# Merge steps dealt at 1.1 a product instead of 2.5, and their dependent transfers moved from the sync queue to GpSimd's queue

## The chip, the cores and the metric

The kernel runs on one core of a Trainium2 chip. The core has five engines that run their own instruction streams in order and meet through semaphores: TensorE (PE in the profile: matmuls; PEld: its weight loads), VectorE (DVE), ScalarE (ACT), GpSimd (POOL) and SyncE (SP, which here only issues transfers). Transfers are issued from an engine's queue (SP's, ACT's or GpSimd's) and carried by 16 DMA engines. The metric is the device time of one execution in microseconds, the median of several runs.

## The reference, cut to what matters

One layer of a decoder step over 1024 prompt tokens and 8 x 4 sample tokens, width 1024, all in float32: an RMS norm, one wide input projection, a gated convolution branch (A), a gated delta-rule branch (B) with 8 heads, two output projections, sigmoid gates, a last projection and a norm. The part that the change touches is in branch B. For each head the tokens are cut in chunks, and each chunk needs the inverse of a unit lower triangular matrix before the chunk-by-chunk scan can start:

```python
M = jnp.where(strict, jnp.einsum('bhnik,bhnjk->bhnij', kb, k) * L, 0.0)
eye = jnp.broadcast_to(jnp.eye(C, dtype=M.dtype), M.shape)
Tm = lax.linalg.triangular_solve(eye + M, eye, left_side=True, lower=True)
u_pre = jnp.einsum('bhnij,bhnjv->bhniv', Tm, vb)
w_dec = jnp.einsum('bhnij,bhnjk->bhnik', Tm, kb * jnp.exp(gc)[..., None])
...
def step(S, inp):
    qd, aqk, kd, up, wd, dl = inp
    u = up - jnp.einsum('bhck,bhkv->bhcv', wd, S)
    o = jnp.einsum('bhck,bhkv->bhcv', qd, S) + jnp.einsum('bhij,bhjv->bhiv', aqk, u)
    S = S * dl[..., None, None] + jnp.einsum('bhck,bhcv->bhkv', kd, u)
    return S, o
```

## The kernel before, in words

The kernel uses chunks of 128 tokens (8 of them) and handles the heads in two groups of 4. First come the norm and the projections of q, k, v and part of the output gate (L287, plain products in three float32r passes). Then the other projections run in pairs of column blocks: `project_pair` computes two blocks in seven smaller products instead of eight. Such a *product* is 24 matmuls of 264 columns (L325). There are 25 pairs, so 175 products: one pair of output gates, four of `C_GB`, sixteen of branch A (`branch_a`), four of `C_GA`. Each product needs a split weight tile `w2`, made by ScalarE (L208) and VectorE (L209) from `wr`, a 512 KB weight tile that SP's queue loads (L174, two per pair, three buffers). `take` prepares the tiles of the next two products ahead. At the end come the two output projections (L287 again) and the last projection with the final norm (L1318).

Beside the products runs the chain of branch B, written as Python generators. `pump`, called after every product, adds `rate[0]` to a credit and takes one generator step per whole credit. `chain` runs four stages one after the other:

- `invert` (two generators, one per head group): inverts the 32 x 32 diagonal blocks on VectorE (L619, L620), then stores them in DRAM (L627, L628, L634, SP's queue).
- `merge` (again one per group): puts the 32-blocks together to 64-blocks and these to 128-blocks, per group in 8 + 8 rounds of two steps. In the first half a round loads `lm`, `lh`, `ll` (L645 to L647), does a small matmul (L671), negates it (L673), a second one (L677), copies it to `xx` (L679) and stores it in the DRAM tensor `tscr` (L682, two transfers). In the second half a round loads `m64` (L652), `rh` and the block-diagonal tile `bd` from `tscr` (L656, L657, two transfers each: these depend on what L627 and L682 stored), does a matmul and two transposes (L693, L695), evacuates them (L697, L699), a second matmul (L703), a copy to `x12` (L705) and a store to `tscr` (L707, two transfers). Loads run one round ahead, through two buffers.
- `scan`: the 8 chunks in order, per group; loads `kt`, `qd`, `av`, `tt`, `kd`, `aqk`, `sz` and stores the output, all on GpSimd's queue (L1107, L1172; `aux` is that queue).
- `sample`: the sample tokens, with `state_in` loads (L965), small matmuls (L1021), state updates (L1091, L1096) and stores (L1098), also on GpSimd's queue.

`rate[0]` is 2.5 from the first product on (L1211) and 1.25 from the scan on (L1204). What is left of the chain is run dry before the last pair (L1221).

The order that is written by these calls isn't the last one: a scheduler that works on estimated times reorders each engine's instructions where dependences allow it. So the program's order on an engine is read from the built program, below.

GpSimd also does one multiplication of branch A (L937, L941) between ScalarE's silu (L954) and VectorE's product with it (L947, L952), and clears and copies the rim of the convolution tile (L907, L909, L926, L927).

Of the kernel before, what the change touches and what calls it, by code (L numbers as in the profile page):

```python
# [31 lines left out]
Q4 = 32  # L32
# [19 lines left out]
def hybrid_step(ctx, tc, x_prompt, x_sample, state_conv_a, state_conv_qkv, state_delta, w_in, conv_a_w,  # L52
                conv_b_w, a_log, dt_bias, onorm_w, w_out_a, w_out_b, w_o, norm_w, final_norm_w,
                y_prompt, y_sample, nca_p, ncq_p, nd_p, nca_s, ncq_s, nd_s):
    nc = tc.nc
    pe, act, dve, pool = nc.tensor, nc.scalar, nc.vector, nc.gpsimd
    aux = nc.gpsimd
# [3 lines left out]
    def opened(**kw):  # L61
        st = ExitStack()
        return st, st.enter_context(tc.tile_pool(reuse_waits="tile", **kw))
# [31 lines left out]
    tscr = dram.tile([2, P, NCH, GH, P], F32, name="tscr")  # L95
# [158 lines left out]
    rate, credit = [1.0], [0.0]  # L254
# [382 lines left out]
    def merge(g, pl):  # L637

        ps_ = potile if g else dtile
        bv = bscr[g].rearrange("(b x c h) a j -> x c (h a) b j", b=2, x=2, c=NCH)  # L640

        def load32(c):
            lm, ll = (pl.tile([P, 2, P], F32, tag=f"{nm}{g}", name=nm, bufs=2) for nm in ("lm", "ll"))
            lh = pl.tile([P, 2, Q4], F32, tag=f"lh{g}", name="lh", bufs=2)
            nc.sync.dma_start(lm, lmscr[g, c])  # L645
            nc.sync.dma_start(lh, bv[1, c])
            nc.sync.dma_start(ll, llscr[g, c])  # L647
            return lm, ll, lh

        def load64(c):  # L650
            m64 = pl.tile([P, 2, P], F32, tag=f"m64{g}", name="m64", bufs=2)
            nc.sync.dma_start(m64, m64scr[g, c])  # L652
            rh = pl.tile([P, 2, 64], F32, tag=f"rh{g}", name="rh", bufs=2)
            for i in range(2):
                half_ = slice(i * 64, (i + 1) * 64)
                nc.sync.dma_start(rh[half_], tscr[g, 64:128, c, i::2, 64:128])  # L656
                nc.sync.dma_start(t1[c % 2][half_, :, half_], tscr[g, 0:64, c, i::2, 0:64])  # L657
            return m64, rh, t1[c % 2]

        nxt = load32(0)  # L660
        t1 = [pl.tile([P, 2, P], F32, name=f"bd{g}{i}") for i in range(2)]
        for t in t1:
            pool.memset(t, 0.0)
        yield
        for c in range(NCH):
            lm, ll, lh = nxt
            if c + 1 < NCH:
                nxt = load32(c + 1)
            pw = ps_()
            for b in range(2):  # L670
                pe.matmul(pw[:, b * Q4:(b + 1) * Q4], lhsT=lm[:, b, :], rhs=lh[:, b, :], start=True, stop=True)  # L671
            ww = pl.tile([P, 2, Q4], F32, tag=f"ww{g}", name="ww")
            dve.tensor_scalar(ww, pw[:, 0:64].rearrange("p (b j) -> p b j", b=2), -1.0, None, op0=ALU.mult)  # L673
            yield
            px = ps_()
            for b in range(2):
                pe.matmul(px[:, b * Q4:(b + 1) * Q4], lhsT=ll[:, b, :], rhs=ww[:, b, :], start=True, stop=True)  # L677
            xx = pl.tile([P, 2, Q4], F32, tag=f"xx{g}", name="xx", bufs=2)
            dve.tensor_copy(xx, px[:, 0:64].rearrange("p (b j) -> p b j", b=2))  # L679
            for b in range(2):  # L680
                o = b * 64
                nc.sync.dma_start(tscr[g, o:o + Q4, c, :, o + Q4:o + 64].rearrange("a h j -> h a j"),  # L682
                              xx[:, b, :])
            yield
        nxt = load64(0)
        yield
        for c in range(NCH):
            m64, rh, tb = nxt
            if c + 1 < NCH:
                nxt = load64(c + 1)  # L690
            pw = ps_()
            for i in range(2):
                pe.matmul(pw[:, i * 64:(i + 1) * 64], lhsT=m64[:, i, :], rhs=rh[:, i, :], start=True, stop=True)  # L693
            for i in range(2):
                pe.transpose(pw[:, P + i * P:2 * P + i * P], tb[:, i, :], ident)  # L695
            w64 = pl.tile([P, 2, 64], F32, tag=f"w64{g}", name="w64")
            dve.tensor_scalar(w64, pw[:, 0:P].rearrange("p (i j) -> p i j", i=2), -1.0, None, op0=ALU.mult)  # L697
            t11 = pl.tile([P, 2, P], F32, tag=f"t11{g}", name="t11")
            act.copy(t11, pw[:, P:3 * P].rearrange("p (i j) -> p i j", i=2))  # L699
            yield  # L700
            px = ps_()
            for i in range(2):
                pe.matmul(px[:, i * 64:(i + 1) * 64], lhsT=t11[:, i, :], rhs=w64[:, i, :], start=True, stop=True)  # L703
            x12 = pl.tile([P, 2, 64], F32, tag=f"x12{g}", name="x12")
            dve.tensor_copy(x12, px[:, 0:P].rearrange("p (i j) -> p i j", i=2))  # L705
            for i in range(2):
                nc.sync.dma_start(tscr[g, 0:64, c, i::2, 64:128], x12[i * 64:(i + 1) * 64])  # L707
            yield

    def potile():  # L710
# [481 lines left out]
    def chain():  # L1192
        for nm, fn in (("iv", invert), ("mg", merge)):
            held, pl = opened(name=nm, bufs=1, side="right")
            live = [fn(g, pl) for g in range(2)]
            while live:
                for one in list(live):
                    try:
                        next(one)
                        yield  # L1200
                    except StopIteration:
                        live.remove(one)
            held.close()
        rate[0] = 1.25  # L1204
        for nm, fn in (("cp", scan), ("sp", sample)):
            held, pl = opened(name=nm, bufs=1, side="right")
            yield from fn(pl)
            held.close()

    background.append(chain())  # L1210
    rate[0] = 2.5  # L1211
    by_pair(C_BZ, 6, AF.Silu, put_z)
# [18 lines left out]
    def htile(pl, nm, n=TT):  # L1231
        return pl.tile([P, n], F32R, tag="h", name=nm)
# [46 lines left out]
    for e in range(KC):  # L1279
        sg = gate_in(gbscr, e)  # L1280
        m = ma[e]
        a, b_ = htile(ha, "mh"), htile(ha, "ml")
# [16 lines left out]
    for k in range(KC):  # L1299
        a, b_ = htile(hb, "woh", D), htile(hb, "wol", D)  # L1300
# [61 lines left out]
```

## Time and profile before

| | us |
|---|---|
| median of 3 runs | 1531.49 (1530.23 to 1535.01) |
| profiled execution | 1535.13 |
| span of its instructions | 1533.4 |
| TensorE busy (matmul) | 1428.1 (93%) |
| VectorE / ScalarE / GpSimd busy | 801.1 / 551.6 / 329.9 |
| mean granted TensorE clock | 0.949 of 2.4 GHz |

The profile is one execution. A view by stretches gives for each engine how long it was busy and, in brackets, how many instructions it began there; PEclk is the clock granted to TensorE as a share of 2.4 GHz. In the timeline an instruction's row ends, where the engine was idle before it, with that idle time and what ended it. "SPq" rows are the issue of transfers on SP's queue; their duration is the time that the issue took, not that of the transfer.

### The profile page before, as it was taken

Reading aid. Unit: us, or ns where it says so; the run is one execution under the profiler, and the core shown is the slowest. Engines: PE = TensorE matmul, PEld = TensorE weight load, DVE = VectorE, ACT = ScalarE, POOL = GpSimd, SP = SyncE. Lnnn points to the kernel's source line nnn. Section 1 sums busy time; section 2 is a strip of 40 time slices with the busy share of each in tenths; the row PEclk is TensorE's granted clock in tenths of the full one; section 3 lists DMA queues with packets and bytes.
Section 4 is the critical chain, followed back from the end, with each engine's and each line's share of the span. In section 5 each row is a group of like instructions: output and inputs, shape, how many; then the busy total and the mean of one; then the engine's idle time right before and its main releaser. Section 6 shows DMA issues by size and latency. Waiting matters only on the chain. (4 is left out here: it accounts for less than half of the span.)

```text
span 1533.4 us, 24570 instructions
## 1 busy us (share of the span) xinstructions
PE 1428.1 (93%) x9673; PEld 1366.6 (89%) x9673; DVE 801.1 (52%) x1456; ACT 551.6 (36%) x1184; POOL 329.9 (22%) x485
## 2 busy tenths in 40 slices
PE   5999898999999998656999999998799999999998
PEld 3899898999999998546999999997799999999885
DVE  6255554435469993213565566467655463255422
ACT  5265564546534431002444444122234460122211
POOL 2032332223211000002565543216200000000200
PEclk9999999999999999557999999799999999999999
DMA  6177656555572345335676564424622283232511
GB/s 192 33 164 209 194 154 191 147 130 145 150 178 85 92 121 144 91 96 157 187 200 200 177 196 137 125 75 143 202 71 86 99 295 112 84 125 86 180 41 45
DMA packets 243077, 212.29 MB, mean 138 GB/s; under 512 B 61417, under 2 KB 215930, under 8 KB 242962
## 3 DMA queue, kind: packets, MB, share of 16 engines
q1 hardware_dynamic: 222272, 143.59, 33.4%
q0 software_dynamic: 17616, 60.37, 13.0%
q10 hardware_dynamic: 3074, 6.77, 1.3%
q8 instruction: 76, 1.25, 0.3%
q14 instruction: 39, 0.32, 0.1%
HBM read 138.12 MB, written 72.56 MB: 137 GB/s over the span
## 5 line engine op out<-in xcount | busy, mean ns | idle before, releaser
L325 PE MATMUL pb<-uh,w 128*128 128x264 f32 x1600 | 315.0, 294 | 17.1 <-ACT w L208 13.7
L325 PEld LDWEIGHTS pb<-uh,w 128*128 128x128 f32 x1600 | 257.6, 194 | 22.7 <-ACT w L208 14.5
L287 PE MATMUL pp<-uh,wl 128*128 128x352 f32 (+1 forms) x744 | 242.9, 326 | 13.5 <-DVE wl L190 13.5
L287 PE MATMUL pp<-uh,wh 128*128 128x352 f32 (+1 forms) x744 | 249.8, 336 | 0.2 <-ACT ext L406 0.2
L287 PE MATMUL pp<-ul,wh 128*128 128x352 f32 (+1 forms) x744 | 242.6, 326 | 0.0
L325 PE MATMUL pb<-ul,w 128*128 128x264 f32 x800 | 233.8, 292 | 0.0
L325 PEld LDWEIGHTS pb<-ul,w 128*128 128x128 f32 x800 | 155.3, 194 | 1.8 <-issue 1.8
L287 PEld LDWEIGHTS pp<-uh,wl 128*128 128x128 f32 (+1 forms) x744 | 140.0, 188 | 17.6 <-DVE wl L190 15.2
L287 PEld LDWEIGHTS pp<-uh,wh 128*128 128x128 f32 (+1 forms) x744 | 139.6, 188 | 4.0 <-issue 0.8
L287 PEld LDWEIGHTS pp<-ul,wh 128*128 128x128 f32 (+1 forms) x744 | 139.9, 188 | 2.0 <-issue 0.5
L208 ACT CAST w<-s 128x512 fp32r<-128x512 f32 x100 | 61.4, 620 | 149.3 <-PE pb L325 65.9
L418 DVE SCALAR_TENSOR_TENSOR cv<-ext,vecT,cv 128x1080 f32<-128x1080 f32 x72 | 99.5, 1386 | 10.1 <-ACT cv L416 8.7
L209 DVE TENSOR_TENSOR w<-s,w 128x512 fp32r<-128x512 f32 x100 | 75.0, 752 | 40.5 <-ACT w L208 39.1
L188 ACT CAST wh<-wr 128x1024 fp32r<-128x1024 f32 (+1 forms) x47 | 48.7, 1036 | 106.8 <-PE pp L287 104.5
L325 PE MATMUL pb<-t4h,w 128*128 128x264 f32 x400 | 81.0, 300 | 6.5 <-DVE p L949 6.5
L209 DVE TENSOR_TENSOR w<-wr,w 128x512 fp32r<-128x512 f32 x75 | 53.0, 709 | 50.9 <-ACT w L208 50.8
L190 DVE TENSOR_TENSOR wl<-wr,wh 128x1024 fp32r<-128x1024 f32 (+1 forms) x47 | 59.8, 1273 | 37.0 <-ACT wh L188 35.5
L325 PE MATMUL pb<-t7h,w 128*128 128x264 f32 x400 | 76.7, 289 | 0.0
L325 PE MATMUL pb<-t6h,w 128*128 128x264 f32 x400 | 76.4, 287 | 0.0
L325 PEld LDWEIGHTS pb<-t4h,w 128*128 128x128 f32 x400 | 65.9, 199 | 7.4 <-issue 7.4
L208 ACT CAST w<-wr 128x512 fp32r<-128x512 f32 x75 | 46.7, 623 | 49.0 <-PE pb L325 44.2
L325 PEld LDWEIGHTS pb<-t7h,w 128*128 128x128 f32 x400 | 63.2, 191 | 0.0
(362 smaller groups left out, 3082.0 us busy)
## 6 DMA issues: line engine op xcount, KB each, us to landing
wr<-in_w_in_dram SPq DMA_DIRECT2D x80, 512.0 KB
scr<-pk SPq DMA_DIRECT2D x16, 768.0 KB
sb<-in_state_delta_dram POOLq DMA_DIRECT2D x16, 512.0 KB, 4.4
zscr<-zt SPq DMA_DIRECT2D x8, 528.0 KB
gbscr<-zt SPq DMA_DIRECT2D x8, 528.0 KB
yscr<-za SPq DMA_DIRECT2D x8, 528.0 KB
gascr<-zt SPq DMA_DIRECT2D x8, 528.0 KB
sg<-gascr POOLq DMA_DIRECT2D x8, 528.0 KB, 4.0
```

What stands on the lines that cost most here:

```text
L188: act.copy(wh, wr)
L190: dve.tensor_tensor(wl, wr, wh.bitcast(F32), op=ALU.subtract)
L208: act.copy(w2[:, 0], src)
L209: dve.tensor_tensor(w2[:, 1], src, w2[:, 0].bitcast(F32), op=ALU.subtract)
L287: pe.matmul(ps[:a.shape[2], :BLK], lhsT=a[:, k, :], rhs=m[k][:, sl], start=(k == 0 and i == 0), stop=(k == KC - 1 and i == 2))
L325: pe.matmul(ps[:, g, :QT], lhsT=a[:, k, :], rhs=m[:, k, sl], start=start and k == 0 and i == 0, stop=(k == 3 and i == 2), skip_group_check ...
L418: dve.scalar_tensor_tensor(cv, ext[:, j:j + LB], vecT[:, j * 24 + ci:j * 24 + ci + 1], cv, op0=ALU.mult, op1=ALU.add)
```

## The change

The rate is set where a stage of the chain begins: 2.5 for `invert`, 1.1 for `merge` (1.25 for the scan and the sample tokens, as before). In `merge` the transfers that store to `tscr` (L682, L707) and the loads that read what such a store wrote (L656, L657) go to GpSimd's queue; `lm`, `lh`, `ll` and `m64` stay on SP's. From L1195 on lines have one number more than before.

```diff
             rh = pl.tile([P, 2, 64], F32, tag=f"rh{g}", name="rh", bufs=2)
             for i in range(2):
                 half_ = slice(i * 64, (i + 1) * 64)
-                nc.sync.dma_start(rh[half_], tscr[g, 64:128, c, i::2, 64:128])
-                nc.sync.dma_start(t1[c % 2][half_, :, half_], tscr[g, 0:64, c, i::2, 0:64])
+                aux.dma_start(rh[half_], tscr[g, 64:128, c, i::2, 64:128])
+                aux.dma_start(t1[c % 2][half_, :, half_], tscr[g, 0:64, c, i::2, 0:64])
...
-                nc.sync.dma_start(tscr[g, o:o + Q4, c, :, o + Q4:o + 64].rearrange("a h j -> h a j"),
+                aux.dma_start(tscr[g, o:o + Q4, c, :, o + Q4:o + 64].rearrange("a h j -> h a j"),
                               xx[:, b, :])
...
-                nc.sync.dma_start(tscr[g, 0:64, c, i::2, 64:128], x12[i * 64:(i + 1) * 64])
+                aux.dma_start(tscr[g, 0:64, c, i::2, 64:128], x12[i * 64:(i + 1) * 64])
...
             held, pl = opened(name=nm, bufs=1, side="right")
+            rate[0] = 2.5 if fn is invert else 1.1
             live = [fn(g, pl) for g in range(2)]
```

**SP's queue, after the stores of `invert`.** Before: the weight tile `wr` for the next pair, then a store of a projection, then the loads of the merges begin.

```order
L634 DMA llscr<-xt 8x32x32 x8
L174 DMA wr<-in_w_in_dram 128x8x128
L1214 DMA gbscr<-zt 128x1056
L645 DMA lm<-lmscr 128x256
L646 DMA lh<-bscr 128x2x32
L647 DMA ll<-llscr 128x256
```

The next weight tile of before stands in the second half of the merges:

```order
L657 DMA bd_5230<-tscr 64x2x64
L656 DMA rh<-tscr 64x2x64
L657 DMA bd_5230<-tscr 64x2x64
L1214 DMA gbscr<-zt 128x1056
L174 DMA wr<-in_w_in_dram 128x8x128
L652 DMA m_6427<-m64scr 128x256
L656 DMA rh<-tscr 64x2x64
```

With the change the same queue has the next weight tile after the first five rounds' loads:

```order
L645 DMA lm<-lmscr 128x256
L646 DMA lh<-bscr 128x2x32
L1215 DMA gbscr<-zt 128x1056
L174 DMA wr<-in_w_in_dram 128x8x128
L645 DMA lm<-lmscr 128x256
L647 DMA ll<-llscr 128x256
```

Between the first of these weight loads and the next, 153 transfers are issued before, and 16 with the change; from there to the end of the merges there are never more than 20 between two.

**TensorE, second half of the merges.** Before, the last first-half rounds and most second-half rounds follow one another with no product between (`pd` and `po` are PSUM tiles of group 0 and group 1, `w64` and `t11` the evacuated results):

```order
L677 MATMUL pd_5911<-ww_5875,ll_5806 128x32 x2
L671 MATMUL po_5906<-lh_5818,lm_5816 128x32 x2
L677 MATMUL po_5948<-ww_5909,ll_5817 128x32 x2
L693 MATMUL pd_6014<-rh_5957,m64_5955 128x64 x2
L695 MATMUL pd_6014<-ident_79,bd00_5229 128x128 x2
L703 MATMUL pd_6069<-w64_6019,t11_6021 128x64 x2
L693 MATMUL po_6030<-rh_5964,m64_5962 128x64 x2
L695 MATMUL po_6030<-ident_79,bd10_5277 128x128 x2
```

With the change the second-half rounds stand between products (L325):

```order
L325 MATMUL pb1_6674<-ul0_121,w2_6586 128x264
L703 MATMUL po_6708<-w64_6628,t11_6630 128x64 x2
L693 MATMUL pd_6752<-rh_6572,m64_6570 128x64 x2
L695 MATMUL pd_6752<-ident_79,bd01_5230 128x128 x2
L693 MATMUL po_6799<-rh_6618,m64_6616 128x64 x2
L695 MATMUL po_6799<-ident_79,bd11_5278 128x128 x2
L325 MATMUL pb1_6674<-t6h_4099,w2_6677 128x264 x2
```

The merges begin at the 37th product in both. They end at the 43rd product before and at the 76th with the change; the scan's first matmul stands in the 46th and in the 82nd, and the last state update of `sample` in the 126th and in the 161st of the 175.

**GpSimd's queue, start of the merges.** Before, nothing of the merges is there:

```order
L663 MEMSET bd_5278 128x256
L907 MEMSET exta 128x2
L909 COPY exta<-pasta 128x8x2
L926 COPY newa<-exta 128x2
L927 COPY newa<-exta 128x16
L907 MEMSET exta 128x2
L909 COPY exta<-pasta 128x8x2
L1107 DMA kt<-scr 128x4x128
```

With the change:

```order
L663 MEMSET bd_5278 128x256
L907 MEMSET exta 128x2
L909 COPY exta<-pasta 128x8x2
L682 DMA tscr<-xx 4x32x32 x4
L657 DMA bd_5229<-tscr 64x2x64 x2
L682 DMA tscr<-xx 4x32x32 x2
L656 DMA rh<-tscr 64x2x64 x2
L657 DMA bd_5277<-tscr 64x2x64
L682 DMA tscr<-xx 4x32x32 x2
L657 DMA bd_5277<-tscr 64x2x64
L656 DMA rh<-tscr 64x2x64 x2
L682 DMA tscr<-xx 4x32x32 x4
```

The stretch of the merges on this queue holds 128 of their transfers and, between them, 21 instructions of branch A.

## Rows read from the trace of the kernel before

**Rows 1.** The page: busy tenths of TensorE, granted clock, in 40 slices.
```profile
PE   5999898999999998656999999998799999999998
PEclk9999999999999999557999999799999999999999
```

**Rows 2.** By stretches: us, busy us (instructions) of each engine, clock, DMA share, GB/s.
```profile
587.80:617.90 30.10, 30.10 (x233) 29.82 (x233) 13.08 (x35) 4.69 (x9) 1.01 (x4) 0.91 0.49 126
632.00:685.00 53.00, 27.57 (x110) 22.36 (x110) 5.74 (x21) 4.71 (x12) 0.00 (x0) 0.50 0.34 87
730.00:940.00 210.00, 208.78 (x1768) 208.34 (x1767) 122.08 (x260) 93.39 (x278) 116.20 (x155) 1.00 0.64 189
940.00:1100.00 160.00, 154.35 (x1072) 143.55 (x1072) 107.83 (x247) 37.62 (x61) 51.86 (x55) 0.91 0.42 124
1100.00:1120.00 20.00, 13.51 (x92) 13.32 (x91) 8.71 (x12) 3.54 (x6) 2.26 (x3) 0.83 0.57 198
```

**Rows 3.** Timeline of SP's queue around the merges: start, duration, instruction.
```profile
581.68 0.41 SPq L174 DMA_DIRECT2D wr<-in_w_in_dram  x1
...
663.57 2.56 SPq L707 DMA_DIRECT2D tscr<-x  x4
...
672.72 2.56 SPq L707 DMA_DIRECT2D tscr<-x  x4
...
679.22 0.43 SPq L174 DMA_DIRECT2D wr<-in_w_in_dram  x1
```

**Rows 4.** Timeline of TensorE around the merges.
```profile
587.74 0.59 PE L325 MATMUL pb<-uh,w 128*128 128x264 f32 x1 [6.18 <-ACT w L208]
...
670.52 1.09 PE L693 MATMUL pd<-rh,m 128*128 128x64 f32 x4 [2.53 <-DMA rh<-tscr]
...
690.74 0.55 PE L703 MATMUL po<-w,t 128*128 128x64 f32 x4
691.29 0.63 PE L693 MATMUL pd<-rh,m 128*128 128x64 f32 x4
691.93 0.41 PE L695 MATMUL pd<-ident,bd 128*128 128x128 f32 x2
...
712.86 0.59 PE L325 MATMUL pb<-uh,w 128*128 128x264 f32 x1 [5.30 <-ACT w L208]
```

**Rows 5.** Stretches, instructions of L325 alone: us, PE busy (count), PEld, clock, DMA.
```profile
594.00:616.00 22.00, 17.17 (x117) 14.96 (x117) 1.00 0.41 99
1160.00:1220.00 60.00, 60.00 (x496) 60.00 (x495) 1.00 0.32 102
581.50:712.80 131.30, 27.91 (x169) 24.53 (x168) 0.65 0.45 116
```

**Rows 6.** The same of 594 to 616, L671 alone, then L677 alone.
```profile
594.00:616.00 22.00, 4.90 (x36) 4.49 (x35) 1.00 0.41 99
594.00:616.00 22.00, 4.82 (x36) 4.80 (x36) 1.00 0.41 99
```

**Rows 7.** GpSimd's transfers: issue in ns (min/median/max); last row, landing of L1172's.
```profile
L1107 POOL DMA_DIRECT2D kt<-scr x16: 747/750/854, 629.4 to 906.3; - x16
L1107 POOL DMA_DIRECT2D tt<-tscr x16: 549/578/627, 704.2 to 912.8; - x16
L1063 POOL DMA_DIRECT2D oscr<-osm x1: 952/952/952, 1040.3 to 1040.3; - x1
DMA to landing us min/median/max: 2.8/3.8/5.8
```

**Rows 8.** Who waited for whom on GpSimd, whole span.
```profile
POOL qd L1107 <- DMA rh<-tscr: 72.4, 1, 72.4
...
POOL sz L1107 <- DMA oscr<-sz: 12.4, 9, 2.5
```

**Rows 9.** Timeline of GpSimd: the multiplication of branch A.
```profile
733.70 1.78 POOL L937 TENSOR_TENSOR za<-za,cv 128x528 f32<-128x528 f32 x1 [0.77 <-ACT za L954]
```

## The prediction

> **What bounds the kernel now.** I read the slices of the page first: TensorE is busy for nine tenths or more nearly everywhere, with one long hole from about 610 to 730 us, and in the same slices the granted clock is halved [rows 1]. So TensorE bounds the kernel, and the question is what the hole holds. The view by stretches cuts it: from 632 to 685 us TensorE is busy 27.6 of 53.0 us at a clock of 0.50, so at 1.2 instead of 2.4 GHz, while the DMA engines are busy only a third of the time [rows 2]. SP's timeline names the holder. A weight tile is issued at 581.68 and the next one at 679.22, 97.5 us later [rows 3]; the order has 153 transfers between them, 0.64 us each, so the queue is full all that time. In the second half of the merges one round of both groups (two `m64`, eight loads, four stores) takes 672.72 - 663.57 = 9.15 us of issue [rows 3]. TensorE, in order, meets a round's matmul and waits for its `rh` (2.53 us in the row shown). Its timeline also shows the ends of the stretch: products wait for their weights until 587.74, after 6.18 us, and again until 712.86, after 5.30 us [rows 4]. Between these lie 131.3 us that hold 169 matmuls of products, seven products and one matmul [rows 5]. After it, from 730 to 940 us, TensorE does products and scan steps at full clock and is busy 208.8 of 210 us [rows 2]: a chain dealt beside products can run without a gap.
>
> **What the change takes away.** The work of the 131.3 us stays; I price it at full clock.
>
> - Products: 60.0 us hold 496 matmuls of L325 where nothing else runs, 0.121 us each [rows 5]. 169 x 0.121 = 20.4 us.
> - First-half matmuls: 594 to 616 us ran at full clock with 117 matmuls of L325, 14.2 us; the other 7.8 us carried 36 + 36 rows of L671 and L677, 18 steps of four rows [rows 5, 6]. 0.435 us a step, 32 steps: 13.9 us.
> - Second-half matmuls: at full clock L703 took 690.74 to 691.29, 0.55 us, and L693 with L695 until 692.34, 1.05 us [rows 4]. Sixteen times 1.60: 25.6 us.
> - The wait of 6.2 us before 587.74 stays: the weight tile that ends it stands behind the same stores of `invert` in both programs.
> - The half clock just after that wait stays: from 587.8 to 617.9 us the granted clock was 0.91 [rows 2], which takes 0.09 x 30.1 = 2.7 us.
>
> Sum: 68.8 us. What goes is 131.3 - 68.8 = 62.5 us. It needs both parts. The rate spreads the merges from the 37th to the 76th product, and the queue's part gives SP back to the weights: no more than 20 transfers, some 13 us at 0.64, between two weight loads.
>
> A rule of the Trainium skill speaks against the second part: "DMA: Bandwidth & Descriptors", section "Issuing engines are not separate DMA queues", says that all queues feed the same 16 DMA engines, so that a second issuing engine only saves issue time, usually a small thing. By that rule alone the queue's part would bring next to nothing. Here the trace differs: issue filled SP's queue for 97.5 us [rows 3] with the DMA engines a third busy [rows 2], so issue time is what is saved.
>
> **What it adds.** 128 transfers on GpSimd's queue. Its trace shows none of this shape; a transfer with 128 rows (`tt`) took 0.58 us to issue, one with 512 rows 0.75, the dearest shown 0.95 [rows 7]. These have 128 rows each, so I take 0.58: 74 us in all, with 0 and 0.95 as ends (122 us). TensorE's own work from the 37th to the 76th product is 40 x 2.91 (24 x 0.121) + 13.9 + 25.6 = 156 us, so the queue is half full. It also carries branch A's multiplications there, six at up to 1.8 us [rows 9]. Stretch 730 to 940 is the nearest row for such a mixture: GpSimd 116 of 210 us busy, TensorE without a gap [rows 2].
>
> The queue works in order, and a load that depends on a store waits on it until the store has landed, 3.8 us after issue [rows 7]. Behind the waiting load stand the next stores, and behind those VectorE's copies to `xx`, which has two buffers a group; behind these PSUM tiles and TensorE. The order exposes one full landing wait, at the first `bd` load; from then on five to nine transfers (3 to 5 us) lie between a store and its load. So one wait is certain, and its delay can reach the first rounds, which TensorE still takes close together. Low end 0, as from 730 to 940; high end one landing for each of six reused buffers, 23 us. I take 5: one landing and a little. In the second half `rh` is loaded six to ten products (17 to 29 us) ahead, no wait.
>
> The scan and the sample tokens move 35 products later, unchanged among themselves. `sample` cost TensorE 5.7 us of idle from 940 to 1100 and 6.5 just after [rows 2]; it now ends beside the `C_GA` pairs, where VectorE has less to do. It may save these 12 us or, with other stores on SP's queue, cost as much again; I take 0. The chain still ends at the 161st product, seven ahead of where it would be run dry.
>
> **Sum.** 1535.1 (the profiled execution, 1.7 us outside the span) - 62.5 + 5 = 1477.6. The profiled execution is 3.6 us above the median of the runs, so 1474.0 on their scale. The forecast's own range: 1535.1 - 62.5 - 12 - 3.6 = 1457 to 1535.1 - 62.5 + 23 + 12 - 3.6 = 1504.
>
> **Rivals.** *GpSimd's queue becomes the chain, and it ends slower.* Place: the first half of the merges. If each of the 16 stores of a round must land before the queue goes on, that is 16 x 3.8 = 61 us, plus the 44 issues that stand there at 0.58, 26: 87 us against TensorE's 12 x 2.91 + 13.9 = 49. TensorE waits 38 us, drops to half clock as it did from 632 to 685, and its 49 us take 98: 1474 - 5 + 38 + 49 = 1556. It decides if most landings are waited for in full. For it: GpSimd has waited on landings, 12.4 us in nine waits in the scan [rows 8]; the 72.4 us there were SP's [rows 8]. Against: the distances in the order.
>
> *VectorE slows GpSimd's issue.* If GpSimd could issue only while VectorE is idle (58% busy from 730 to 940 [rows 2]), 0.58 becomes 1.38 us, 128 of them 177 and branch A's 10: 187 against 156, so 31 us of waits, 1500. Against: `kt` took 747 to 854 ns in just that stretch, hardly any spread [rows 7]. The Trainium skill, "SBUF — State Buffer", section "Who interferes with whom", says that VectorE's copies in two-port modes lock GpSimd out while it writes descriptors; the trace shows at most 0.1 us of that.
>
> *Weights stay late.* SP still has 64 loads of the merges, which wait for buffers in order. If every pair from the 43rd product to the 84th loses what the wait of 5.3 us and its half clock (2.7) cost: 6 x 8 = 48 us, 1522. Both loads of each pair: 1570. Against: no load in front of a weight tile waits for a matmul later than the weight's own place.
>
> *The steps only move.* If the chain can't finish in time, `sample`'s state updates run without products. Before they stand beside the 118th to the 126th product, 8 x 2.91 = 23 us that would be uncovered: 1497. The order, with the last of them at the 161st product, speaks against it.
>
> **Chances.** Forecast 0.78; GpSimd's chain 0.05; VectorE's lock 0.05; late weights 0.08 (a quarter of it with both loads, slower, and a quarter between, no change); moved only 0.04. A measurement can tell 0.3%, 4.6 us. Faster: 0.78 + 0.05 + 0.04 + 0.04 = 0.91, less 0.01 for ends of these beyond; no change 0.03; slower 0.07. The range 1457 to 1504 holds the forecast and two rivals, over 8 in 10.
>
> **What would show it.** Right: no gap of more than 35 us between weight loads on SP's queue; TensorE's clock at 1.0 from 600 us on until the sample stage; no waits of L693 on `rh` and of L703 on its evacuation; L1107's first scan rows near 790 us; GpSimd's issues of L656, L657, L682 and L707 at about 0.58 us. Wrong: waits of L671 or L677 on VectorE's L679, and these on landings; GpSimd rows above 1.2 us; L208 waiting for weights at every pair; VectorE's L947 or L952 waiting for L937.

## The result, and the profile after

The changed kernel took 1458.91 us (median of 3 runs, 1457.01 to 1459.33) against 1531.49: a ratio of 0.9518, 95% interval 0.9490 to 0.9546. It lies inside the range given, near its lower end, 15 us below the forecast. In the profiled executions the span fell from 1533.4 to 1457.2 us, 76.2 us where the sum had 57.5.

The slices of the changed kernel, in which nothing is left of the hole and of the halved clock beside it [rows 1]:

```profile
PE   4999898998999999899999999999999899999998
PEclk8999999999999999999999999999999999999999
```

The view by stretches of the changed kernel, for the stretches of [rows 2]. The columns are the length, the busy time of PE, PEld, DVE, ACT and POOL with the instructions begun, the granted clock, the DMA engines' share and GB/s:

```profile
587.80:617.90 30.10, 25.60 (x192) 24.64 (x193) 15.35 (x38) 6.36 (x11) 16.20 (x26) 0.89 1.00 254
632.00:685.00 53.00, 52.31 (x438) 51.96 (x438) 29.12 (x55) 17.82 (x32) 31.90 (x54) 1.00 0.39 94
730.00:940.00 210.00, 206.35 (x1734) 206.16 (x1733) 119.54 (x247) 87.99 (x250) 116.51 (x161) 0.99 0.63 180
940.00:1100.00 160.00, 159.44 (x1218) 151.91 (x1217) 102.75 (x242) 50.44 (x106) 57.71 (x62) 0.97 0.48 142
1100.00:1120.00 20.00, 19.61 (x139) 17.13 (x138) 11.85 (x28) 6.37 (x11) 7.33 (x7) 1.00 0.74 240
```

In the stretch from 632 to 685 us TensorE was busy 27.6 of 53.0 us at a clock of 0.50; it is now busy 52.3 at 1.00, and begins 438 matmuls there.

SP's timeline of the changed kernel, weight tiles alone, where 97.5 us lay between two of them [rows 3]:

```profile
584.82 0.41 SPq L174 DMA_DIRECT2D wr<-in_w_in_dram  x1
594.75 0.38 SPq L174 DMA_DIRECT2D wr<-in_w_in_dram  x1
...
607.88 0.42 SPq L174 DMA_DIRECT2D wr<-in_w_in_dram  x1
632.97 6.17 SPq L174 DMA_DIRECT2D wr<-in_w_in_dram  x2
658.99 0.38 SPq L174 DMA_DIRECT2D wr<-in_w_in_dram  x1
```

The widest gap up to the end of the merges is 25 us (607.88 to 632.97). What TensorE still waits for from 590 us to the end of the products (line, releaser, us in total, times, longest):

```profile
PE pb L325 <- ACT w L208: 5.5, 1, 5.5
PE pb L325 <- DVE p L858: 5.0, 1, 5.0
PE pb L325 <- DVE cs L916: 3.6, 1, 3.6
PE pb L325 <- ACT p L331: 1.4, 2, 0.7
```

Of the merges' own matmuls only L671 and L677 wait, 1.3 us together, for plain loads on SP's queue. The second and third row name VectorE, but they are late weights. VectorE, in order, stood before each of them in L198, its first step on the second weight tile of a pair, until that tile had landed (VectorE's timeline; the product waits until 767.84 and 1136.25):

```profile
765.87 0.69 DVE L198 TENSOR_TENSOR s<-wr 128x512 f32<-128x512 f32 x1 [6.50 <-DMA wr<-in_w_in_dram]
767.08 0.70 DVE L916 TENSOR_TENSOR cs<-pb,u 128x528 f32<-128x528 f32 x1
...
1133.59 0.69 DVE L198 TENSOR_TENSOR s<-wr 128x512 f32<-128x512 f32 x1 [5.55 <-DMA wr<-in_w_in_dram]
1135.40 0.70 DVE L858 TENSOR_TENSOR p<-pb,p 128x528 f32<-128x528 f32 x1
```

One sum serves the whole study. From the first product behind the wait for weights (587.7 us before, 591.0 after) to the last matmul of the products (1238.2 and 1161.7) I added up, in stretches of 10 us, the time in which TensorE was idle, and the time that it was busy times what its clock lacked to 1.00. The rest is work at full clock. Where the slices are cut moves the half clock by about 1 us, so the last two columns are no finer than that.

| kernel | median | ratio, 95% interval | length | idle | half clock | rest |
|---|---|---|---|---|---|---|
| before | 1531.49 | | 650.5 | 56.9 | 43.1 | 550.5 |
| changed | 1458.91 | 0.9518 (0.9490 to 0.9546) | 570.7 | 12.3 | 10.2 | 548.2 |
| changed, once more | 1457.67 | 0.9523 (0.9497 to 0.9548) | 569.1 | 11.4 | 9.9 | 547.8 |
| rate alone | 1468.09 | 0.9596 (0.9567 to 0.9625) | 582.9 | 13.0 | 24.2 | 545.7 |
| queue alone | 1483.70 | 0.9695 (0.9670 to 0.9720) | 596.9 | 23.4 | 24.2 | 549.3 |
| second half twice | 1468.72 | 0.9601 (0.9564 to 0.9638) | 584.7 | 9.8 | 11.5 | 563.4 |
| `invert`'s store on GpSimd | 1461.82 | 0.9543 (0.9513 to 0.9574) | 576.0 | 14.8 | 10.7 | 550.6 |
| rate 1.5 | 1468.91 | 0.9603 (0.9581 to 0.9625) | 581.7 | 18.1 | 14.6 | 549.0 |
| rate 0.9 | 1472.93 | 0.9627 (0.9607 to 0.9646) | 549.5 | 2.0 | 5.4 | 542.1 |
| stores alone | 1450.50 | 0.9481 (0.9461 to 0.9502) | 566.5 | 7.9 | 13.3 | 545.4 |
| stores alone, once more | 1449.59 | 0.9472 (0.9450 to 0.9495) | 567.3 | 8.3 | 14.3 | 544.7 |
| loads alone | 1457.67 | 0.9513 (0.9492 to 0.9534) | 566.9 | 9.3 | 11.5 | 546.1 |
| stores alone, rate 1.2 | 1461.78 | 0.9540 (0.9515 to 0.9565) | 572.0 | 15.2 | 7.5 | 549.3 |
| all on GpSimd | 1491.03 | 0.9729 (0.9706 to 0.9753) | 601.3 | 28.0 | 22.4 | 551.0 |

The rest is nearly the same everywhere (at 0.9 part of the work stands behind the products, and with the second half twice there is more of it). So the change removed 44.6 us of idle time and 32.9 of half clock, 77.5 of 79.8 us. What lies ahead of this stretch differs by up to 6 us between the profiled executions, between two of one kernel as well (the product that begins at 475.0 us in one starts at 478.9 in the other), so single profiles can't be compared more closely than that over the whole span. Each ratio is to runs of the kernel before on the same chip in the same rounds.

### The profile page after: what moved, and what is told of

Same layout as the page of the kernel before. It is cut to its first block, busy times and chain, and to the rows that moved or that the text cites. A ratio compares the mean times of both kernels' runs of the same rounds, so it can differ in the third digit from the quotient of the medians.

```text
span 1457.2 us, 24544 instructions
## 1 busy us (share of the span) xinstructions
PE 1393.4 (96%) x9673; PEld 1339.5 (92%) x9673; DVE 793.8 (54%) x1456; ACT 550.9 (38%) x1184; POOL 408.6 (28%) x613
## 3 DMA queue, kind: packets, MB, share of 16 engines
q8 instruction: 76, 1.25, 0.3%
## 4 chain that ended last, share of the span: by engine, by line
PE 68%; DMA 12%; DVE 11%; issue 3%; SPq 3%; POOL 1%; ACT 1%; DVEq 0%; POOLq 0%; ACTq 0%
PE pb L325 27%; PE pp L287 24%; PE pp L1319 6%; DMA ee<-gscr 6%; DMA wr<-in_w_in_dram 2%; DVE cv L418 2%; DMA sb<-in_state_delta_dram 1%; DVE wl L190 1%; DMA ya<-in_x_prompt_dram 1%; DVE xi L620 1%; PE pd L1021 1%; DVE pr L619 1%; PE po L1147 1%; PE pd L1145 1%; PE pd L756 1%
## 5 line engine op out<-in xcount | busy, mean ns | idle before, releaser
L325 PE MATMUL pb<-uh,w 128*128 128x264 f32 x1600 | 312.1, 292 | 12.1 <-ACT w L208 5.8
L325 PEld LDWEIGHTS pb<-uh,w 128*128 128x128 f32 x1600 | 253.5, 191 | 17.3 <-ACT w L208 7.2
L325 PE MATMUL pb<-ul,w 128*128 128x264 f32 x800 | 232.1, 290 | 0.0
L325 PEld LDWEIGHTS pb<-ul,w 128*128 128x128 f32 x800 | 153.1, 191 | 1.7 <-issue 1.7
L208 ACT CAST w<-s 128x512 fp32r<-128x512 f32 x100 | 61.5, 620 | 139.1 <-PE pb L325 97.8
L209 DVE TENSOR_TENSOR w<-s,w 128x512 fp32r<-128x512 f32 x100 | 72.2, 723 | 32.6 <-ACT w L208 32.2
L325 PE MATMUL pb<-t4h,w 128*128 128x264 f32 x400 | 78.8, 295 | 5.0 <-DVE p L858 5.0
L325 PE MATMUL pb<-t7h,w 128*128 128x264 f32 x400 | 77.6, 291 | 0.0
L325 PE MATMUL pb<-t6h,w 128*128 128x264 f32 x400 | 77.2, 289 | 0.0
L325 PEld LDWEIGHTS pb<-t4h,w 128*128 128x128 f32 x400 | 64.2, 194 | 6.4 <-issue 6.4
L208 ACT CAST w<-wr 128x512 fp32r<-128x512 f32 x75 | 46.7, 623 | 52.5 <-PE pb L325 50.2
L331 ACT COPY p<-pb 128x528 f32<-128x528 f32 x50 | 30.0, 600 | 92.7 <-PE pb L325 92.7
```

Of the source, the lines that this page charges most:

```text
L208: act.copy(w2[:, 0], src)
L209: dve.tensor_tensor(w2[:, 1], src, w2[:, 0].bitcast(F32), op=ALU.subtract)
L325: pe.matmul(ps[:, g, :QT], lhsT=a[:, k, :], rhs=m[:, k, sl], start=start and k == 0 and i == 0, stop=(k == 3 and i == 2), skip_group_check ...
L331: act.copy(t, ps)
```

## The experiments

My theory was the prediction's: the hole needs both parts to go, since SP's queue is full. The rival: one part alone is enough, because dealing the merges out also spreads SP's transfers.

**The rate alone** (the kernel before with the one line):

```diff
             held, pl = opened(name=nm, bufs=1, side="right")
+            rate[0] = 2.5 if fn is invert else 1.1
```

> The rate of 1.1 alone; all transfers of the merges stay on SP's queue. Theory A (the full SP queue keeps the weight tiles from TensorE, so both parts are needed): the merges are spread over the 37th to the 76th product, but the order has 58 transfers in front of the third weight tile of the stretch (37 us at 0.64) and 14 to 22 in front of every second one after, with stores that wait for their copies in order: 1495 us, between 1480 and 1515, with L208 waiting for weights several times. Theory B (only the bunching cost, the queue doesn't matter): 1459, within 7 us. A weight gap of 37 us or more on SP's queue belongs to A.

Measured: 0.9596, 1468.09 us, outside both ranges (A's 1480 to 1515, B's 1452 to 1466) and much nearer to B's. The theory falls: the rate alone brings 4.0% of the 4.8. But A's sign, a weight gap of 37 us, is there. SP's timeline, weight tiles again:

```profile
596.59 0.38 SPq L174 DMA_DIRECT2D wr<-in_w_in_dram  x1
633.79 0.38 SPq L174 DMA_DIRECT2D wr<-in_w_in_dram  x1
636.90 0.50 SPq L174 DMA_DIRECT2D wr<-in_w_in_dram  x1
```

One gap of 37 us is left of 97.5, with 58 transfers in it. By stretches, first that place and then two of the sample tokens' stage, which the edit doesn't touch:

```profile
628.00:648.00 20.00, 14.39 (x80) 13.50 (x81) 7.63 (x17) 3.75 (x7) 0.00 (x0) 0.66 0.50 125
...
1010.00:1030.00 20.00, 20.00 (x141) 19.52 (x140) 10.55 (x31) 1.86 (x3) 4.45 (x6) 0.83 0.42 124
1030.00:1050.00 20.00, 19.37 (x101) 19.16 (x99) 5.56 (x7) 2.92 (x4) 2.65 (x3) 0.58 0.39 114
```

In the first, 10 merge matmuls stand without a product in front of the 44th. It costs 11.0 us: ten products that took 39.1 us with both parts take 50.1 here. The others are busy at a lower clock: that stage holds 9 of the 14 us by which half clock here exceeds the changed kernel's (16.5 us from 995 us to the end of the products, against 7.1 from 985 there).

**The queue alone** (the changed kernel without that line):

```diff
-            rate[0] = 2.5 if fn is invert else 1.1
```

> The queue's part alone; the merges are dealt at 2.5 a product as before. Theory A: the order has 43 transfers in front of the next weight tile (some 28 us) and 22 rows of merge matmuls without a product at the 53rd product, then the queue is free: 1475 us, 1463 to 1490, most of the gain. Theory B (the bunching costs): 1510 or more. Theory C (the queue alone is all of it): 1459, within 7 us.

Measured: 0.9695, as expected. The waits of L693 for `rh` are gone, but 22 merge matmuls still stand in front of the 53rd product with no product between, and these wait for the chain of their own evacuations (waits, then the stretch):

```profile
PE po L703 <- ACT t L699: 5.7, 4, 3.2
...
665.00:695.00 30.00, 21.50 (x107) 18.85 (x106) 6.87 (x21) 3.95 (x11) 26.42 (x45) 0.60 0.43 119
```

The ten products there take 61.2 us, 26 more than with both parts. Alone the parts bring 4.0% and 3.05%, together 4.8: they remove largely the same hole. Neither run isolates its part, though: each edit also changes the order that the scheduler makes. The longest runs of merge matmuls without a product are 46 and 13 before, 22 with the queue alone, 10 with the rate alone and at most 5 with both.

**The second half of the merges twice** (in the changed kernel; each matmul of L693, L695 and L703 writes its tile twice):

```diff
-            for i in range(2):
-                pe.matmul(pw[:, i * 64:(i + 1) * 64], lhsT=m64[:, i, :], ...)
...
+            for _ in range(2):
+                for i in range(2):
+                    pe.matmul(pw[:, i * 64:(i + 1) * 64], lhsT=m64[:, i, :], ...)
...
```

> As with the change, but each matmul and transpose of the second half (L693, L695, L703) is issued twice, with the same result. It measures the price of a round: if a round costs TensorE 0.94 us, as the trace with the change has it, 15 us more than the changed kernel, 1474; if it costs 1.60, as the prediction priced it from a stretch at full clock, 26 us more, 1485. If TensorE weren't the bound there, less than 5 us.

Measured: 0.9601, and the rest in the table grows from 548.2 to 563.4: 15.2 us for 16 rounds, 0.95 us a round. The rest of the kernels with the same work lies between 544.7 and 551.0, so this is good to about 0.2 us a round. The prediction's 1.60 a round is refuted.

**`invert`'s store to `llscr` on GpSimd's queue** (in the changed kernel), against the wait of 5.5 us that stayed:

```diff
-                nc.sync.dma_start(lv[h, b, :, :, h * Q4:(h + 1) * Q4], xt[...])
+                aux.dma_start(lv[h, b, :, :, h * Q4:(h + 1) * Q4], xt[...])
```

> As with the change, and the sixteen small stores of invert (L634) go to GpSimd's queue. The weight tile that stands behind them is issued some 11 us earlier. Theory A: the wait of 5.5 us before the 37th product and the half clock after it (2.7) go, 1451 us, 8 less than with the change. Rival: the wait only moves, to the first loads of the merges that need these stores or to the second weight tile: 1456 to 1461.

Measured: 0.9543, no gain. L208's wait is down to 0.3 us, but a wait of 6.9 us stands at 589.7 us, where L208's was. The profile puts it to L858, yet VectorE stood in L198 until 587.61, for the weight tile. That tile was issued 4.9 us earlier than in the changed kernel, not 11, and with the next pair's tile 1.3 us behind it; it took 7.6 us to land instead of 4.7 (the chain of the changed kernel, then this one's chain and its VectorE):

```profile
584.82 4.67 DMA wr<-in_w_in_dram
...
579.96 7.63 DMA wr<-in_w_in_dram
...
587.61 0.69 DVE L198 TENSOR_TENSOR s<-wr 128x512 f32<-128x512 f32 x1 [9.99 <-DMA wr<-in_w_in_dram]
```

So the wait for weights stayed, under another name. The rival has the number nearly right (1456 to 1461, measured 1461.82), but the wait did not move to either of its two places.

From the first two runs I formed a new theory: what costs is a run of merge matmuls that stand in the order without a product, some 1.1 us a row, whichever queue carries the transfers.

**Rate 1.5** (in the changed kernel, 1.1 to 1.5):

```diff
-            rate[0] = 2.5 if fn is invert else 1.1
+            rate[0] = 2.5 if fn is invert else 1.5
```

> The changed kernel with 1.5 a product in place of 1.1 (both queues as changed). In the order 15 matmuls of L693, L695 and L703 then stand behind the 53rd product with no product between them; 27 transfers are the most between two weight loads on SP. Theory A (what costs is a run of dependent steps without products, whichever queue carries their transfers): the two runs seen so far cost 10.3 us for 10 rows (rate alone) and 26.1 us for 22 rows (queue alone), so about 1.1 us a row, 15 rows 16 us: 1475 us (1468 to 1482), with a hole of about 15 us at the 53rd product and the clock below 1.0 in it. Theory B (the prediction's: SP's full queue is what costs; with GpSimd carrying 128 of the transfers a run without products costs nothing): 1459 us (1454 to 1464).

Measured: 1468.91 us, at the lower end of theory A. In front of the 53rd product ten products take 53.5 us in place of 35.1, so the 15 rows cost 18 us there, but 7 of them come back later (the length in the table is 11 us more).

**Rate 0.9** (the same line):

```diff
-            rate[0] = 2.5 if fn is invert else 1.1
+            rate[0] = 2.5 if fn is invert else 0.9
```

> The changed kernel with 0.9 a product in place of 1.1. The merges reach to the 89th product, the scan from the 93rd to the 141st, and the sample tokens' state updates from the 169th to the 175th, the last. Theory A (spreading gains until no run of merge steps stands alone; beyond that it only moves the end of the chain towards the last product): 1462 us (1457 to 1470). Rival, the prediction's fourth (steps that no product covers any more come back at the end): what follows the state updates stands alone, up to 8 x 2.91 = 23 us: 1476 to 1482. Theory C (more spreading still gains): under 1455.

Measured: 1472.93 us, theory A missed, and the rival's 1476 to 1482 as well. The middle is the cleanest of all (idle 2.0, half clock 5.4), and the products end 22 us earlier, at 1139.5; but then the sample tokens' last steps stand alone. TensorE's wait there, and the stretch around it:

```profile
PE pp L287 <- ACT yh L1237: 32.2, 1, 32.2
...
1140.00:1180.00 40.00, 7.81 (x23) 5.63 (x22) 12.01 (x29) 6.28 (x7) 6.11 (x8) 0.59 0.89 324
```

This is the rival "the steps only move" at its place, but not by its price. TensorE's last state updates there take 3.6 us. Most of the 32.2 us are three transfers, one behind the other, on the chain: the store of a state, the load of the last state behind it, and the load of the next products' input behind that state's update:

```profile
1142.62 11.93 DMA out_dram<-sb
1154.84 7.46 DMA sb<-in_state_delta_dram
...
1166.07 8.24 DMA y<-yscr
```

At 1.1 the same tail is still covered, with seven products to spare.

**The stores alone on GpSimd's queue** (the changed kernel with the loads back on SP's):

```diff
-                aux.dma_start(rh[half_], tscr[g, 64:128, c, i::2, 64:128])
-                aux.dma_start(t1[c % 2][half_, :, half_], tscr[g, 0:64, c, i::2, 0:64])
+                nc.sync.dma_start(rh[half_], tscr[g, 64:128, c, i::2, 64:128])
+                nc.sync.dma_start(t1[c % 2][half_, :, half_], tscr[g, 0:64, c, i::2, 0:64])
```

> The changed kernel with the dependent loads (L656, L657) back on SP's queue; only the stores L682 and L707 stay on GpSimd's. No run of merge steps stands without products in the order; SP has up to 36 transfers between two weight loads (20 before this edit). Theory A (only runs without products cost): no loss against the changed kernel, 1459 us (1454 to 1464). Theory B (a gap between weight loads costs: 36 transfers at 0.64 us are 23 us, and the rate alone had 58 and 37 us for a loss of 9 us): about half of that loss, 1464 us, with a wait of L208 for its weights beyond the first of 5.5 us.

Measured: 1450.50 us, ratio 0.9481, below both theories.

**All of the merges' transfers on GpSimd's queue** (the changed kernel with `lm`, `lh`, `ll` and `m64` there too):

```diff
-            nc.sync.dma_start(lm, lmscr[g, c])
-            nc.sync.dma_start(lh, bv[1, c])
-            nc.sync.dma_start(ll, llscr[g, c])
...
-            nc.sync.dma_start(m64, m64scr[g, c])
+            aux.dma_start(lm, lmscr[g, c])
+            aux.dma_start(lh, bv[1, c])
+            aux.dma_start(ll, llscr[g, c])
...
+            aux.dma_start(m64, m64scr[g, c])
```

> The changed kernel with the merges' plain loads (lm, lh, ll, m64: 64 transfers) on GpSimd's queue as well, so that it carries all 192 and SP none. 192 x 0.6 = 115 us of issue stand beside 156 us of TensorE's own work. The order then has 19 merge matmuls behind the 53rd product without a product between. Theory A (the run without products costs, about 1.1 us a row): 1459 + 20 = 1479 us (1472 to 1486). Theory B (SP's queue is what costs, and it is now empty): 1459 us or a little less (1453 to 1463). Rival, the prediction's first (GpSimd's queue in order becomes the chain, waits for landings with more behind them): 1490 us or more, with waits of POOL on landings of over 20 us.

Measured: 1491.03 us, above theory A and where the rival put it (1490 or more). The rival's cause is not there: GpSimd waits for no landing from 655 to 690 us. The queue has one transfer behind the other, and the stretch is a hole at a clock of 0.61 (GpSimd's timeline, then the stretch, then what TensorE waited for from 655 to 690 us):

```profile
674.19 0.63 POOL L656 DMA_DIRECT2D rh<-tscr  x1
674.79 0.61 POOL L657 DMA_DIRECT2D bd<-tscr  x1
675.37 0.61 POOL L656 DMA_DIRECT2D rh<-tscr  x1
675.94 0.62 POOL L657 DMA_DIRECT2D bd<-tscr  x1
...
652.00:687.00 35.00, 24.63 (x130) 22.64 (x130) 8.84 (x25) 3.23 (x7) 31.45 (x53) 0.61 0.43 104
...
PE po L677 <- DVE ww L673: 3.6, 3, 3.0
PE pd L693 <- DMA rh<-tscr: 1.9, 1, 1.9
PE po L693 <- issue: 1.7, 1, 1.7
PE po L695 <- DMA bd<-tscr: 1.0, 1, 1.0
```

GpSimd is busy 31.5 of 35 us there, but two things add up. Ten products take 63.9 us in place of 35.0, 29 more, of which 19 bare rows at 1.1 would be 21. Of TensorE's 10.4 us of idle time 2.9 are waits for `rh` and `bd`, 1.7 have no releaser in the profile, and the others are the chain's own evacuations. That the full queue makes the other 8 us fits, but is not isolated. SP carries nothing of the merges here and still has 50 us between two weight tiles (654.38 to 704.42), so a weight gap alone doesn't show a full queue.

**Changed and stores alone, once more, side by side.** No edit:

> The changed kernel once more, beside the kernel with the stores alone on GpSimd's queue, since their ratios so far are from different rounds (0.9518 and 0.9481, with intervals that touch). If the difference is real: 1457 to 1460 us here against 1449 to 1453 there. If it was the rounds': both within 4 us of each other.

> The stores alone on GpSimd's queue (L656 and L657 on SP's), once more. Real difference: 1450 us (1448 to 1453), 6 to 9 us below the changed kernel. No difference: within 4 us of it.

Measured: 1457.67 and 1449.59 us, ratios 0.9523 (0.9497 to 0.9548) and 0.9472 (0.9450 to 0.9495). The difference is there again, 8 us, the intervals just apart. **The loads alone** on GpSimd's queue (the stores back on SP's):

```diff
-                aux.dma_start(tscr[g, o:o + Q4, c, :, o + Q4:o + 64].rearrange("a h j -> h a j"),
+                nc.sync.dma_start(tscr[g, o:o + Q4, c, :, o + Q4:o + 64].rearrange("a h j -> h a j"),
...
-                aux.dma_start(tscr[g, 0:64, c, i::2, 64:128], x12[i * 64:(i + 1) * 64])
+                nc.sync.dma_start(tscr[g, 0:64, c, i::2, 64:128], x12[i * 64:(i + 1) * 64])
```

> The other half of the queue's part: the dependent loads L656 and L657 on GpSimd's queue, the stores L682 and L707 back on SP's. In the order 10 merge matmuls stand behind the 44th product with no product between, as with the rate alone, and 6 behind the 65th; 58 transfers stand between two weight loads on SP. Theory A (runs without products cost, about 1.1 us a row): the stores give all of the queue's part and the loads nothing, so as the rate alone or a little over: 1468 us (1463 to 1477). Theory B (any 64 transfers taken from SP do the same): 1459 us or less, as with the stores.

Measured: 1457.67 us, ratio 0.9513, the changed kernel's. The 10 rows in front of the 44th product cost what they cost with the rate alone (ten products in 50.6 us), and 58 transfers and 35.8 us lie between two weight tiles again, so theory A is right at the place; but the part from the 80th product to the last took 391.4 us against 404.4 in the changed kernel and 406.3 with the rate alone. Neither a price per bare row nor the weight gap therefore gives the time.

**Stores alone at 1.2** (as the stores alone, with 1.2 in the rate line):

```diff
-            rate[0] = 2.5 if fn is invert else 1.1
+            rate[0] = 2.5 if fn is invert else 1.2
```

> The stores alone on GpSimd's queue and 1.2 a product in place of 1.1. In the order no run of merge matmuls stands without products; the merges end at the 70th product in place of the 76th, the sample tokens' state updates at the 156th in place of the 161st. Theory A: as with 1.1, 1450 us (1446 to 1455), since no row is bare in either. Theory B (the less is dealt a product, the better, as long as the chain ends beside the products): 1455 to 1462, on the way to the 1469 of 1.5.

Measured: 1461.78 us, 12 us worse than at 1.1, with no row of the merges bare. Theory A misses, theory B's number fits; its cause isn't shown. The longest waits are one put to branch A, which is again a late weight tile, and one for the state updates (waits, then VectorE's timeline):

```profile
PE pb L325 <- DVE u L949: 5.3, 1, 5.3
PE pd L1091 <- DVE sb L1096: 2.2, 1, 2.2
...
741.13 0.69 DVE L198 TENSOR_TENSOR s<-wr 128x512 f32<-128x512 f32 x1 [8.19 <-DMA wr<-in_w_in_dram]
```

## Why the prediction was right, and where it was not

**The mechanism held.** The hole was merge steps with no products beside them, and the time came back as idle time and half clock, 77.5 us of them. What TensorE waited for in the hole before:

```profile
PE pd L693 <- DMA rh<-tscr: 17.3, 6, 5.3
PE po L703 <- ACT t L699: 6.9, 7, 1.9
PE pd L703 <- ACT t L699: 6.7, 8, 0.8
```

Two waits for weights there make 7.2 us more. L693 no longer waits for `rh`, nor L703 for its evacuation; the clock is at 1.00 from 632 to 685 us; the wait before the first weight tile stayed (6.2 us before, 5.5 after). With the queues as changed and 1.5 in place of 1.1 the hole is back, so spreading the steps is what closes it.

**"It needs both parts" failed.** The rate alone brings most of it, and the queue alone most of that again. The prediction counted the 153 transfers between two weight tiles as a property of the queue, but they stood there because the merges were dealt in seven products. Spread over 40 products the 192 transfers of the merges are 192 x 0.64 = 123 us of issue beside its own 156 us of TensorE work: SP could carry them all. Both numbers stood in the prediction; the division was made for GpSimd alone. The time could not tell: the forecast, 1474.0, lies nearer to the rate alone (1468) than to both parts (1459), and the measured time is 2 us inside the range's end, by errors that partly cancel, as the next paragraphs show.

**The second-half round was mis-sized**: 1.60 us, 25.6 for 16; measured 0.95 and 15.2, so 10.4 us of the 22 that the sum was short. The prediction read it from one round in the hole [rows 4]. TensorE's timeline of the changed kernel has the same rows between products:

```profile
688.60 0.55 PE L703 MATMUL pd<-w,t 128*128 128x64 f32 x4
688.96 0.48 PE L325 MATMUL pb<-t7h,w 128*128 128x264 f32 x2
...
703.26 0.61 PE L693 MATMUL pd<-rh,m 128*128 128x64 f32 x4
703.70 0.39 PE L695 MATMUL pd<-ident,bd 128*128 128x128 f32 x2
703.85 0.37 PE L325 MATMUL pb<-t6h,w 128*128 128x264 f32 x1
```

L703 lasts 0.55 us here too, but the next row starts 0.36 us after it; L693 and L695 together take 0.59 from start to start, where the prediction had 1.05. What a row costs among others is the distance to the next start. The prediction also counted L695 to its end, 0.41 us, where the next start comes 0.15 us after its own. Why L703's distance was 0.55 in that one row no run isolates: the clock was already 1.00 (690 to 692 us), and with the queue alone L693 starts 0.39 us after L703 with no product between (664.31 us, clock 1.00).

**First-half steps and new waits.** 32 steps were given 13.9 us; from start to start they take 13.7. The wait for a landing (5 us taken, 0 to 23) came to nothing: GpSimd waits 3.6 us on landings of `tscr` and `rh` in all, and no matmul of the merges waits for it.

**GpSimd's issue** was 0.58 us by its nearest row [rows 7]. The lines of the changed kernel (instances; minimum, median and maximum in ns; first and last start):

```profile
L682 POOL DMA_DIRECT2D tscr<-xx x32: 687/693/796, 598.1 to 649.8; - x32
...
L657 POOL DMA_DIRECT2D bd<-tscr x32: 585/606/645, 603.0 to 711.0; - x32
...
L707 POOL DMA_DIRECT2D tscr<-x x32: 590/596/629, 653.0 to 749.7; - x32
```

0.60 for three of the four kinds, 0.69 for L682, 80 us in all for the 74. It was hidden, as the term said, but the margin is thin: with 64 transfers more the hole is back (1491). VectorE's lock does not show: L657's rows spread by 60 ns and L682's by 109, while VectorE is busy 55% of the time. The section "Who interferes with whom" of "SBUF — State Buffer" in the Trainium skill speaks of such a lock; no run here shows it.

**The sample tokens' stage** was given 0 (-12 to +12). From 712.9 us to the end of the products before, and from 745.5 after, idle time went from 13.5 to 9.6 us and half clock from 18.0 to 8.3 (17.9 and 9.3 when cut where the clock changes): 12.5 to 13.6 us less, at the bound or just past it. The 12 us that the prediction read as the cost of `sample` were in part late weights: the longest of these waits, 6.5 us at 1110.3 us, stands behind VectorE's L198:

```profile
1107.64 0.69 DVE L198 TENSOR_TENSOR s<-wr 128x512 f32<-128x512 f32 x1 [8.92 <-DMA wr<-in_w_in_dram]
```

With the second-half rounds (10.4) and the landing (5) that makes 28 to 29, and the sum was short by 22 (in the stretch, 79.8 against 57.5). What went the other way is a product among steps: from 588 to 785 us 1199 matmuls of L325 take 154.1 us from start to start, 9.0 more than at the 0.121 that they were given. The sample tokens' stage is what differs most between the variants, too, and I didn't isolate why its clock falls: TensorE is busy nearly without a gap when it does.

**The rule that was weighed.** "DMA: Bandwidth & Descriptors" in the Trainium skill, section "Issuing engines are not separate DMA queues", holds the issue time that a second engine saves for usually small beside the transfer itself. The queue's part brought 12 us on top of the rate's 62 (0.9596 to 0.9518, of 1531 us), and 47 by itself (0.9695). It was small once the rate had spread the transfers, and not small while they stood together; how much of the 47 is issue time and how much the new order is not isolated.

**The signs named.** L1107's first rows, expected near 790, came at 750.3 us. After the first wait L208 has none over 1 us, but late weights did show, under other names: the waits of 3.6 us at 767.8 and of 5.0 us at 1136.3 end with a weight tile. So that rival came true for two pairs behind the merges, far from its price. The clock drops to 0.50 from 769.1 to 772.5 us, right behind the first of these waits.

**The best of the kernels** has only the stores on GpSimd's queue. Of its 8 us the stretch in the table holds 1.8 to 4.2 (the late weight tile near 768 us is gone); the rest lies where two executions of one kernel differ by as much, so where it comes from stays open.

## What to carry to other kernels

When steps of a chain are bunched, look first at how they are dealt out: spread over more matmul work, the full queue beside them empties as well, and one number did most of what two changes did. Divide each queue's issue time by the time over which the new order spreads it, for the old queue and for the new one, before moving transfers; and leave the end of the chain some products of cover, since at 0.9 a product the cleanest middle of all gave its whole gain back in one wait of 32 us. Price a matmul that will stand among others by the distance to the next start, not by the duration of a row. And where the profile puts a wait to an engine that works in order, look at what that engine waited for itself: five waits of products here, named after VectorE's later steps, were late weight tiles.

## What was not expected of the hardware

- The granted clock falls in the sample tokens' stage while TensorE is busy nearly all the time, with products and the small matmuls of L1021: 20.00 of 20 us at 0.83, then 19.37 of 20 at 0.58 with the rate alone. The half clock from 995 us to the end of the products was 16.5 us there and 2.8 from 990 us with the loads alone, the chief difference between two kernels whose merges stand nearly alike.
- Two stores with the same number of rows take GpSimd different times to issue: 0.69 us for L682 (32 elements a row), 0.60 for L707 (64 elements a row).
- The four small matmuls of L703 show 0.55 us in a row at full clock, but the next start comes 0.36 us after theirs when it is a product's and mostly 0.39 when it is another merge row's; 0.55 to the next start stood once, in the round that the prediction read.
